# Loading the first tile of a ragged layer norm by a plain GpSimd transfer instead of an indexed gather

## The chip, the cores and the metric

The kernel runs on one core of a Trainium2 chip. Its time is device microseconds (us) of one execution. Before the change, three runs took 264.95, 263.61 and 265.17 us; the median is 264.95 us. The profiled execution is one of them.

The engines are named as in the profile: PE is the matrix engine (TensorE), PEld its weight load, DVE the vector engine, ACT the scalar engine, POOL is GpSimd, SP the sync engine. Sixteen DMA engines move the data between the memory (HBM) and the core's buffers.

## The reference

`x` holds 32 batches of 512 rows of 1,024 float32 values. Of each batch only the first `lengths[b]` rows count (64 to 511, drawn once); they are normalised, scaled by `gamma` and shifted by `beta`, and all other rows of the output are zero.

```python
output = np.zeros_like(x)
for b in range(batch):
    seq_len = lengths[b]
    x_b = x[b, :seq_len].copy()
    mean = np.mean(x_b, axis=-1, keepdims=True)
    var = np.var(x_b, axis=-1, keepdims=True)
    x_norm = (x_b - mean) / np.sqrt(var + eps)
    output[b, :seq_len] = x_norm * gamma + beta
```

## The kernel before

**Units and tiles.** Four consecutive rows of a batch are a unit: 16 KiB, contiguous in memory (`UR = 4`, line 14). A tile is 128 units, one in each partition, 2 MiB. Every batch has at least 64 rows, so the first 16 units of each batch are always valid: these 512 units are the four static tiles (`NST = 4`; tile 0 holds the first 64 rows of batches 0 to 7, `BPT = 8`). The units behind the first 16 of each batch are valid as far as the length says. The kernel counts the valid ones through all batches and packs them densely into dynamic tiles; the units that hold no valid row are packed likewise into zero tiles. The drawn lengths give 1,814 valid dynamic units, so 14 full dynamic tiles and one partial tile with 22 units.

**Loads and stores.** All of them are indirect transfers issued by GpSimd (lines 521, 540 and 547): each of the 128 partitions has the number of its unit in a column of an index tile, and a number out of range is left out. The static tiles take their numbers from `sidx`, which a short chain makes: an iota for the partition number `p_i` and one for the tiles' bases `sb_i` on GpSimd (lines 178 and 179), a shift and a multiply-add on DVE (lines 180 to 184). The dynamic tiles take theirs from `idx_i`, the end of a longer chain on DVE that starts with the lengths (lines 231 to 267). The zero tiles are scattered from one zeroed buffer, `zt`, with numbers from `zidx`. In the partial tile the order of units over the partitions is permuted (lines 202 to 213): the low four bits of a unit's place are bits 2, 3, 4 and 6 of the partition's number.

**The order of work.** The program of each engine is written out by hand: `add` appends an instruction with its semaphore waits, and `raw` appends a marker to GpSimd's list, such as `("load", 0)`. GpSimd's own block (from line 501) walks the list and turns these markers into transfers. It is in order: the two iotas, the loads of tiles 0 and 1, more iotas, the identity's memset, loads 2 to 7, the memset of `zt`. Before load 0 it waits for `sidx` (line 558), before load 4 for `idx_i` and for the number of tiles (lines 559 to 564). After that comes a loop over the tiles: store tile t once it is evacuated, scatter one zero tile at the steps listed in `ZSTEPS`, load tile t + 7 into the buffer that has come free (there are eight buffers, `R = 8`). What zero tiles are left follow at the end.

**The compute** goes by half tiles, two units' rows at a time. DVE takes the statistics from `x` (line 362) and the small reciprocals (lines 352, 353), ACT normalises into a half-precision buffer `h` (line 373), DVE multiplies by gamma (line 346), PE carries `h` over by an identity matrix and adds beta by a rank-one product (lines 398 and 404), ACT evacuates the sum with the row mask into the same `x` buffer (line 382), from which the store goes out.

Of the kernel before, what the change touches and what calls it, by code (L numbers as in the profile page):

```python
# [13 lines left out]
UR = 4  # L14
ST_ROWS = 64
# [6 lines left out]
class Program:  # L22
# [10 lines left out]
    def add(self, eng, fn, deps=(), inc=True):  # L33
        know = self.know[eng]
        waits = {}
        for dep in deps:
            if dep is None:
                continue
            key, val = dep
            if key == eng:  # L40
                waits[key] = max(waits.get(key, 0), val)
                continue
            if know.get(key, 0) >= val:
                continue
            waits[key] = max(waits.get(key, 0), val)
            know[key] = max(know.get(key, 0), val)
            for k2, v2 in self.snap.get(dep, {}).items():
                if k2 != eng:
                    know[k2] = max(know.get(k2, 0), v2)
        own = waits.pop(eng, None)  # L50
        if own is not None and know.get(eng, 0) < own:
            waits[eng] = own
            know[eng] = own
        if inc:
            self.count[eng] += 1
            token = (eng, self.count[eng])
            self.snap[token] = {k: v for k, v in know.items() if k != eng}
        else:
            token = None
        self.ops[eng].append(("op", fn, list(waits.items()), inc))  # L60
        return token
# [8 lines left out]
def kernel(tc, x, lengths, gamma, beta, eps, out):  # L70
# [6 lines left out]
    BPT = B // NST  # L77
# [10 lines left out]
    s_x = [tc.alloc_semaphore(f"s_x{i}") for i in range(R)]  # L88
# [10 lines left out]
    with pool_cm as sb, psum_cm as psb:  # L99
        def st(shape, dt, name):  # L100
            return sb.tile(shape, dt, name=name)

        xt = [st([P, UR * D], FP32, f"x{i}") for i in range(R)]
# [66 lines left out]
        pr = Program(sem)  # L170
        add = pr.add

        def iota(t, pattern, base=0, mult=0):
            return add("POOL", lambda: pool.iota(t, pattern=pattern, base=base, channel_multiplier=mult,
                                                 allow_small_or_imprecise_dtypes=True))


        a_p = iota(p_i[:, :], [[0, 1]], 0, 1)
        a_sb = iota(sb_i[:, :], [[BPT * U, NST]], 0, 1)
        a_p4 = add("DVE", lambda: dve.tensor_scalar(out=p4_i[:, :], in0=p_i[:, :], scalar1=4, scalar2=None,  # L180
                                                    op0=OP.logical_shift_right), [a_p])
        a_sidx = add("DVE", lambda: dve.scalar_tensor_tensor(
            out=sidx[:, :], in0=p4_i[:, 0:1].broadcast_to([P, NST]), scalar=float(U - S0), in1=sb_i[:, :],
            op0=OP.mult, op1=OP.add), [a_p4, a_sb])
        pr.raw("POOL", ("load", 0))
        pr.raw("POOL", ("load", 1))
        a_q = iota(q_f[:, :], [[P, NQ]], 0, 1)
        a_t = iota(t_f[:, :], [[1, NQ]])
# [5 lines left out]
            out=idn_f[:, :], in_=idn_f[:, :], compare_op=OP.not_equal, fill=1.0,  # L194
# [235 lines left out]
        def emit_op(e, name, op):  # L430
            _, fn, waits, inc = op
            for key, val in waits:
                e.wait_ge(handles[key], val)
            ins = fn()
            if inc:
                ins.then_inc(sem[name], 1)
# [8 lines left out]
        def tiles_register(e, r):  # L445

            e.reg_add(r, r, P - 1)
            e.reg_alu(r, r, 7, OP.arith_shift_right)
            e.reg_add(r, r, NST)
# [28 lines left out]
        with tc.tile_critical():  # L478
            with nc.Block() as block:

                @block.vector
                def _(e):
                    run_engine(e, "DVE", block)
# [17 lines left out]
                @block.gpsimd  # L501
                def _(e):
                    base = nc.cur_bb
                    rt = rb = None
                    guard = None

                    def goto(name):
                        nonlocal guard
                        if guard is not None:
                            guard.__exit__(None, None, None)  # L510
                        guard = nc.bb(name, parent=base)
                        guard.__enter__()

                    def wait(dep):
                        e.wait_ge(handles[dep[0]], dep[1])

                    def column(t):
                        return sidx[:, t : t + 1] if t < NST else idx_i[:, t - NST : t - NST + 1]

                    def load(t):  # L520
                        e.indirect_dma_start(
                            out=xt[t % R][:, :], out_offset=None, in_=xu,
                            in_offset=bass.IndirectOffsetOnAxis(ap=column(t), axis=0),
                            bounds_check=B * U - 1, oob_is_err=False).then_inc(s_x[t % R], 16)

                    def guarded_load(t):
                        if t <= NST:
                            load(t)
                            return
                        e.br_lt(rt, t, f"POOL_n{t}", f"POOL_l{t}")  # L530
                        goto(f"POOL_l{t}")
                        if t >= R:
                            wait((f"o{t % R}", 16 * (t // R)))
                        load(t)
                        e.br(f"POOL_n{t}")
                        goto(f"POOL_n{t}")

                    def store(t):
                        wait(tok["evac", 2 * t + 1])
                        e.indirect_dma_start(  # L540
                            out=ou, out_offset=bass.IndirectOffsetOnAxis(ap=column(t), axis=0),
                            in_=xt[t % R][:, :], in_offset=None,
                            bounds_check=B * U - 1, oob_is_err=False).then_inc(s_o[t % R], 16)

                    def zero(j):
                        g = NZ - 1 - j
                        e.indirect_dma_start(  # L547
                            out=ou, out_offset=bass.IndirectOffsetOnAxis(ap=zidx[:, g : g + 1], axis=0),
                            in_=zt[:, :], in_offset=None,
                            bounds_check=B * U - 1, oob_is_err=False).then_inc(s_zero, 16)  # L550

                    for op in pr.ops["POOL"]:
                        if op[0] == "op":
                            emit_op(e, "POOL", op)
                            continue
                        t = op[1][1]
                        if t == 0:
                            wait(a_sidx)
                        if t == NST:
                            wait(d_idx)  # L560
                            rt = units_register(e, "POOL")
                            rb = e.alloc_register("POOL_rb")
                            e.reg_alu(rb, rt, 7, OP.arith_shift_right)
                            tiles_register(e, rt)
                        guarded_load(t)

                    def ready(j):
                        if j == 0:
                            wait(d_zidx)
                            wait(a_zt)  # L570

                    j = 0
                    for t in range(NT):
                        store(t)
                        if t in ZSTEPS and j < NZ:
                            ready(j)
                            e.br_lt(rb, NZ - j, f"POOL_z{t}", f"POOL_y{t}")
                            goto(f"POOL_z{t}")
                            zero(j)
                            e.br(f"POOL_y{t}")  # L580
                            goto(f"POOL_y{t}")
                            j += 1
                        if t >= 1 and t - 1 + R <= NT:
                            guarded_load(t - 1 + R)
                        if t >= NST - 1 and t < NT - 1:
                            e.br_lt(rt, t + 2, f"POOL_e{j}", f"POOL_s{t + 1}")
                            goto(f"POOL_s{t + 1}")
                    e.br(f"POOL_e{j}" if j < NZ else "POOL_exit")
                    for j in range(NZ):
                        goto(f"POOL_e{j}")  # L590
                        ready(j)
                        e.br_lt(rb, NZ - j, f"POOL_t{j}", "POOL_exit")
                        goto(f"POOL_t{j}")
                        zero(j)
                        e.br(f"POOL_e{j + 1}" if j + 1 < NZ else "POOL_exit")
                    goto("POOL_exit")
                    e.drain()
                    e.br(block.end_bb)
                    guard.__exit__(None, None, None)
# [35 lines left out]
```

## Time and profile before

| | |
|---|---|
| median of three runs | 264.95 us |
| profiled execution, in all | 264.95 us |
| span of the profiled execution, first to last instruction | 263.2 us |
| busy: ACT, DVE, PE, POOL | 69%, 67%, 54%, 23% of the span |
| moved by DMA | 105.42 MB in 7,795 packets, 401 GB/s over the span |
| read from and written to HBM | 41.98 MB and 69.21 MB |
| first load, from issue to landing | 8.5 us |
| loads of the second round, from issue to landing | 17.6 to 25.6 us |
| last zero scatter issued | 227.70 us |

The page's second part cuts the span into 40 equal slices, 6.58 us each; a digit is the busy share of that slice in tenths, for the engines and for the mean of the 16 DMA engines. The third part lists the DMA queues with their packets, megabytes and the time that their packets took as a share of 16 engines' span. The timeline lists instructions in order: start, duration, engine, line, operation, output and inputs, and in brackets the idle time of the engine before it and what ended it. A table of stretches gives the busy time of each engine in a part of the span, the granted clock, the share of the DMA engines and GB/s. [...]

### The profile page before, as it was taken

Reading aid. Unit: us, or ns where it says so; the run is one execution under the profiler, and the core shown is the slowest. Engines: PE = TensorE matmul, PEld = TensorE weight load, DVE = VectorE, ACT = ScalarE, POOL = GpSimd, SP = SyncE. Lnnn points to the kernel's source line nnn. Section 1 sums busy time; section 2 is a strip of 40 time slices with the busy share of each in tenths; the row PEclk is TensorE's granted clock in tenths of the full one; section 3 lists DMA queues with packets and bytes.
Section 4 is the critical chain, followed back from the end, with each engine's and each line's share of the span. In section 5 each row is a group of like instructions: output and inputs, shape, how many; then the busy total and the mean of one; then the engine's idle time right before and its main releaser. Section 6 shows DMA issues by size and latency. Waiting matters only on the chain.

```text
span 263.2 us, 1571 instructions
## 1 busy us (share of the span) xinstructions
PE 141.7 (54%) x306; PEld 32.4 (12%) x306; DVE 177.2 (67%) x411; ACT 182.9 (69%) x198; POOL 61.7 (23%) x67
## 2 busy tenths in 40 slices
PE   1006546466687587677767866875876777000000
PEld 0001111111111111111111111111111111000000
DVE  5899796967688778868887886887788688000000
ACT  5144938577989989998998999899899989300000
POOL 5590030315043040302202401240207611200000
DMA  3999999999999999999999999999999999999940
GB/s 111 391 410 406 433 431 431 431 431 433 406 436 408 418 427 421 431 431 428 428 426 426 433 420 423 435 421 428 423 431 428 421 431 416 421 422 426 431 209 10
DMA packets 7795, 105.42 MB, mean 401 GB/s; under 512 B 1356, under 2 KB 1356, under 8 KB 1358
## 3 DMA queue, kind: packets, MB, share of 16 engines
q0 software_dynamic: 7632, 105.22, 95.1%
q8 instruction: 4, 0.07, 0.1%
q14 instruction: 11, 0.09, 0.1%
q10 hardware_dynamic: 148, 0.04, 0.1%
HBM read 41.98 MB, written 69.21 MB: 423 GB/s over the span
## 4 chain that ended last, share of the span: by engine, by line
DVE 35%; PE 27%; ACT 17%; DMA 3%; issue 3%; POOL 0%; ACTq 0%; DVEq 0%; POOLq 0%; SPq 0%
DVE stats_127 L362 17%; PE ps_144 L398 14%; PE ps_144 L404 13%; DMA x_61<-in_x_dram,sidx 3%; DVE h_69 L346 3%; DVE h_71 L346 3%; DVE h_70 L346 3%; ACT x_63 L382 3%; ACT x_62 L382 2%; ACT x_61 L382 2%; ACT x_67 L382 2%; ACT x_68 L382 2%; ACT x_66 L382 2%; ACT x_65 L382 2%; ACT x_64 L382 2%
## 5 line engine op out<-in xcount | busy, mean ns | idle before, releaser
L404 PE MATMUL ps_144<-row_h,ones_h 1*128 1x512 f16 x76 | 35.8, 622 | 0.0
L404 PE MATMUL ps_145<-row_h,ones_h 1*128 1x512 f16 x76 | 35.8, 622 | 0.0
L398 PE MATMUL ps_144<-h_69,idn_h 128*128 128x512 f16 x28 | 13.2, 628 | 26.7 <-DVE h_69 L346 26.7
L398 PE MATMUL ps_144<-h_71,idn_h 128*128 128x512 f16 x24 | 11.3, 627 | 15.5 <-DVE h_71 L346 15.5
L398 PE MATMUL ps_144<-h_70,idn_h 128*128 128x512 f16 x24 | 11.3, 627 | 13.8 <-DVE h_70 L346 13.8
L398 PE MATMUL ps_145<-h_70,idn_h 128*128 128x512 f16 x28 | 13.2, 627 | 6.8 <-DVE h_70 L346 6.8
L346 DVE TENSOR_TENSOR h_69<-h_69,gamma_h 128x2048 f16<-128x2048 f16 x13 | 15.5, 1191 | 1.0 <-ACT x_63 L382 1.0
L547 POOL DMA_INDIRECT out_dram<-zt,zidx x14 | 14.3, 1024 | 5.2 <-issue 3.7
L346 DVE TENSOR_TENSOR h_70<-h_70,gamma_h 128x2048 f16<-128x2048 f16 x13 | 15.4, 1187 | 0.0
L398 PE MATMUL ps_145<-h_71,idn_h 128*128 128x512 f16 x24 | 11.3, 627 | 6.6 <-DVE h_71 L346 6.6
L398 PE MATMUL ps_145<-h_69,idn_h 128*128 128x512 f16 x24 | 11.3, 628 | 6.5 <-DVE h_69 L346 6.5
L346 DVE TENSOR_TENSOR h_71<-h_71,gamma_h 128x2048 f16<-128x2048 f16 x12 | 14.3, 1192 | 0.0
L404 PEld LDWEIGHTS ps_144<-row_h,ones_h 1*128 1x128 f16 x76 | 7.9, 125 | 26.6 <-issue 26.6
L404 PEld LDWEIGHTS ps_145<-row_h,ones_h 1*128 1x128 f16 x76 | 7.9, 125 | 26.6 <-issue 26.6
L352 DVE RECIPROCAL rstd_138<-sq_134 128x2 f32<-128x2 f32 x10 | 1.7, 166 | 13.7 <-ACT sq_134 L389 13.7
L352 DVE RECIPROCAL rstd_136<-sq_132 128x2 f32<-128x2 f32 x10 | 1.7, 166 | 12.9 <-ACT sq_132 L389 12.9
L362 DVE BATCH_NORM_STATS2 stats_126<-x_61 128x6 f32<-128x512 f32 x12 | 7.4, 679 | 0.9 <-DMA x_61<-in_x_dram,sidx 0.9
L398 PEld LDWEIGHTS ps_144<-h_69,idn_h 128*128 128x128 f16 x28 | 3.0, 131 | 36.8 <-DVE h_69 L346 33.0
L362 DVE BATCH_NORM_STATS2 stats_127<-x_63 128x6 f32<-128x512 f32 x12 | 7.4, 680 | 0.0
L362 DVE BATCH_NORM_STATS2 stats_127<-x_62 128x6 f32<-128x512 f32 x12 | 7.4, 679 | 0.0
L362 DVE BATCH_NORM_STATS2 stats_126<-x_64 128x6 f32<-128x512 f32 x12 | 7.4, 679 | 0.0
L362 DVE BATCH_NORM_STATS2 stats_126<-x_62 128x6 f32<-128x512 f32 x12 | 7.4, 678 | 0.0
(181 smaller groups left out, 356.9 us busy)
## 6 DMA issues: line engine op xcount, KB each, us to landing
out_dram<-zt,zidx POOLq DMA_INDIRECT x14, 26.5
len_73<-in_lengths_dram ACTq DMA_DIRECT2D x1, 32.0 KB, 2.9
x_65<-in_x_dram,idx_i POOLq DMA_INDIRECT x2, 22.0
x_66<-in_x_dram,idx_i POOLq DMA_INDIRECT x2, 21.4
x_67<-in_x_dram,idx_i POOLq DMA_INDIRECT x2, 23.9
x_68<-in_x_dram,idx_i POOLq DMA_INDIRECT x2, 25.6
x_61<-in_x_dram,idx_i POOLq DMA_INDIRECT x2, 19.1
x_62<-in_x_dram,idx_i POOLq DMA_INDIRECT x2, 21.0
```

Source lines behind the costliest of these rows:

```text
L346: tok["mul", t] = add("DVE", lambda: dve.tensor_tensor(out=h[:, :, :], in0=h[:, :, :], in1=gamma_h[:, None, :].broadcast_to([P, 2, D]), op ...
L352: a = add("DVE", lambda: dve.reciprocal(out=rstd[r][:, :], in_=sq[r][:, :]), [tok["sqrt", t]])
L362: tk = add("DVE", lambda j=j, c=c: dve.bn_stats(out=s[:, j, c, :], in_=xx[:, j * D + c * CH : j * D + c * CH + CH]), [load_dep(t // 2)])
L382: tok["evac", t] = add("ACT", lambda j=j, row=row: act.activation(out=xx[:, j * D : j * D + D], in_=p_[:, j, :], func=AF.Copy, bias=0.0, s ...
L398: add("PE", lambda j=j, c=c: pe.matmul(p_[:, j, c * CH : c * CH + CH], idn_h[:, :], h[:, j, c * CH : c * CH + CH], start=True, stop=False) ...
L404: tok["pe", t] = add("PE", lambda j=j, c=c: pe.matmul(p_[:, j, c * CH : c * CH + CH], ones_h[:, :], row_h[:, D + c * CH : D + c * CH + CH] ...
L547: e.indirect_dma_start(out=ou, out_offset=bass.IndirectOffsetOnAxis(ap=zidx[:, g : g + 1], axis=0), in_=zt[:, :], in_offset=None, bounds_c ...
```

## The change

The marker `("load", 0)` is moved up between the two iotas, and GpSimd's block issues that load as a plain transfer that takes no indices: the source is the first 64 rows of batches 0 to 7, regrouped into 8 batches of 16 units of 4,096 elements, the destination the whole buffer, 128 partitions. The wait for `sidx` moves from load 0 to load 1. The bytes moved and their places are the same. No other engine's instructions change.

```diff
         a_p = iota(p_i[:, :], [[0, 1]], 0, 1)
+        pr.raw("POOL", ("load", 0))
         a_sb = iota(sb_i[:, :], [[BPT * U, NST]], 0, 1)
         a_p4 = add("DVE", lambda: dve.tensor_scalar(out=p4_i[:, :], in0=p_i[:, :], scalar1=4, scalar2=None,
                                                     op0=OP.logical_shift_right), [a_p])
         a_sidx = add("DVE", lambda: dve.scalar_tensor_tensor(
             out=sidx[:, :], in0=p4_i[:, 0:1].broadcast_to([P, NST]), scalar=float(U - S0), in1=sb_i[:, :],
             op0=OP.mult, op1=OP.add), [a_p4, a_sb])
-        pr.raw("POOL", ("load", 0))
         pr.raw("POOL", ("load", 1))
...
                         t = op[1][1]
                         if t == 0:
+                            e.dma_start(out=xt[0][:, :],
+                                        in_=x[0:BPT, 0:ST_ROWS].rearrange("b (p r) d -> b p (r d)", r=UR)
+                                        ).then_inc(s_x[0], 16)
+                            continue
+                        if t == 1:
                             wait(a_sidx)
                         if t == NST:
                             wait(d_idx)
```

## The prediction

> **What bounds the kernel now.** I read the page from its top. In the second part I look for an engine at 9 in every slice, and in the third at what each queue carries.
>
> ```profile
> DMA  3999999999999999999999999999999999999940
> GB/s 111 391 410 406 433 431 431 431 431 433 406 436 408 418 427 421 431 431 428 428 426 426 433 420 423 435 421 428 423 431 428 421 431 416 421 422 426 431 209 10
> ...
> q0 software_dynamic: 7632, 105.22, 95.1%
> ```
>
> No compute engine does that (ACT, the busiest, is at 69%), but the DMA engines do from the second slice to the 38th, almost all of it in one queue, the one that GpSimd fills. So the time is the start of the transfers, plus the bytes on the engines, plus the end. The price of a tile comes from the last line: 105.22 MB are 6,422 pieces of 16 KiB; 0.951 x 16 x 263.2 us = 4,005 engine-us, hence 0.624 us a piece. A tile of 128 rows is 79.8 engine-us, or 4.99 us when dealt evenly to 16 engines.
>
> The chain that ended last starts with the first tile's load and then walks through DVE, PE and ACT. It must not be taken for the bound: the last store and the last zero scatter are issued at 226.42 and 227.70 us, and the engines still move over 400 GB/s until 251 us. Some 25 us of transfers are waiting in the queue when the compute is done. The start is in the timeline of GpSimd:
>
> ```profile
> 1.06 0.13 POOL L174 IOTA p_i<- 128x1 int32 x1 [0.62 <-SPq L479]
> 1.15 0.12 POOL L174 IOTA sb_i<- 128x4 int32 x1
> 2.62 1.18 POOL L521 DMA_INDIRECT x_61<-in_x_dram,sidx  x1 [1.35 <-DVE one_106 L216]
> 4.11 1.00 POOL L521 DMA_INDIRECT x_62<-in_x_dram,sidx  x1 [0.30 <-issue]
> ```
>
> The first gather is issued at 2.62 us, 0.97 us after its indices are done (DVE writes `sidx` from 1.49 to 1.65). Its issue takes 1.18 us, and it lands 8.5 us after the start of it (sixth part of the page), at 11.13. The end is in stretches of 1 us, where the last two columns are the mean busy share of the 16 engines and GB/s:
>
> ```profile
> 251.00:252.00 1.00, 0.00 (x0) 0.00 (x0) 0.00 (x0) 0.00 (x0) 0.00 (x0) 1.00 0.78 328
> 252.00:253.00 1.00, 0.00 (x0) 0.00 (x0) 0.00 (x0) 0.00 (x0) 0.00 (x0) 1.00 0.61 262
> 253.00:254.00 1.00, 0.00 (x0) 0.00 (x0) 0.00 (x0) 0.00 (x0) 0.00 (x0) 1.00 0.46 197
> 254.00:255.00 1.00, 0.00 (x0) 0.00 (x0) 0.00 (x0) 0.00 (x0) 0.00 (x0) 1.00 0.35 147
> 255.00:256.00 1.00, 0.00 (x0) 0.00 (x0) 0.00 (x0) 0.00 (x0) 0.00 (x0) 1.00 0.08 33
> 256.00:257.00 1.00, 0.00 (x0) 0.00 (x0) 0.00 (x0) 0.00 (x0) 0.00 (x0) 1.00 0.04 16
> ...
> 258.00:259.00 1.00, 0.00 (x0) 0.00 (x0) 0.00 (x0) 0.00 (x0) 0.00 (x0) 1.00 0.04 16
> ```
>
> A share of 0.04 to 0.08 is one engine of sixteen. The engines don't help each other out: from 256 us one of them works alone. The kernel ends with **the most loaded or slowest engine**, not with the mean. The trace's records of the single semaphore increments (each transfer has sixteen) say the same: those of the last scatter arrive from 252.08 to 256.10 us and one, the last, at 259.62; 3.5 us of barrier and exit follow to the span's 263.2.
>
> **The change part by part.** The sum is made against the profiled execution, 263.2 us of span and 264.95 us in all, which is also the median of the runs shown.
>
> (1) *The first load no longer waits for indices.* Both kernels issue it as GpSimd's first transfer; now it follows the `p_i` iota, done at 1.19. How late it starts after that is not shown. The smallest gap ahead of any issue in the timeline is 0.30 us, the gap of the first issue of all is the 0.97 above, part of which may be waiting. So it starts at 1.49 to 2.16 instead of 2.62: 0.46 to 1.13 us gained. I take 0.46, since the row of the first issue is the nearest. The issue of a plain transfer on GpSimd isn't in the trace either: the nearest rows are the gather's 1.18 us and, as ends, 0.23 us (a plain issue on ACT, L490) and 2.00 us (the longest indirect one). I take 1.18, no change; the ends are 0.95 gained and 0.82 lost. Together **-0.46 us**, between -2.08 and +0.36. As the queue is never empty afterwards, the start moves the end by as much.
>
> (2) *`sb_i` is now queued behind the issue on GpSimd*, so it is written near 2.16 + 1.18 = 3.4 us, not 1.15, and `sidx` near 3.7, not 1.49. Behind `sidx` on DVE stand the ten small operations of lines 204 to 216 (1.57 to 2.67 us); they end near 4.8. The lengths' cast follows (3.82 before, 1.0 us later now), and so does the index chain, whose `idx_i` is done at 11.1 in place of 10.09; ACT's first activation waits for one of these constants, `row_h` stands behind it, and `gamma_h` slips with them. Cover: load 1 waits for `sidx` and is issued at 4.0 to 4.6 (4.11 before) while the first tile is still moving; load 4 (11.70 before, it needs `idx_i`) finds loads 1 to 3 queued, 15 us of work; `gamma_h` is first used at 20.70. Cost 0; without the cover of the queue it would be 1.0 us.
>
> (3) *How the tile is dealt to the engines.* The gather takes 128 rows of 16 KiB by index. The plain transfer's source, `x[0:8, 0:64]` regrouped, is a pattern of three dimensions: 8 batches, 16 units in each, 4,096 elements; the batches can't be merged with the units, since 448 rows lie between. No row of before shows a plain transfer of this size. The nearest are ACT's: the lengths' broadcast, 128 rows, goes as 128 packets, while gamma, one row of 4.0 KB, is a single packet on a single engine (the page counts only two packets between 2 and 8 KB: gamma and beta). So a plain transfer is dealt by the shape of its pattern, not by its bytes. Two ends, then: all 128 rows over 16 engines, +0; or the eight outer blocks over eight engines, 16 pieces each. By the second the eight carry 8 pieces more than before, 8 x 0.624 = **+4.99 us**, and the other eight as much less. I take eight, because the outermost dimension is what differs from the gather's pattern, and gamma's row shows that a single outer block isn't split.
>
> [...]
>
> (4) *Whether the last engine is among the eight.* In the code the partial tile's units are permuted (lines 202 to 213), its 22 valid units (the drawn lengths give 1,814, or 14 x 128 + 22) going one to each of sixteen groups of partitions and a second one to the first six. The engine that lands last, at 259.62, took 1.21 us for the store of that tile, two pieces, where ten engines took one; so it is one of the first six, and all partitions of those lie below 64. Eight engines counted from the first would include it. I take that: the whole 4.99 counts.
>
> Load 0 then lands some 5 us later than 2.16 + 8.5, near 15.6, and the compute starts 4.5 us late (first statistics at 11.15 before). That is hidden: the last scatter would be issued at 232 and the queue runs to 264. The queue's smallest stock is ahead of store 1 (47.92), which lands after 13.4 us, 4.99 of them its own: 8.4 us. On the loaded engines stock and issue shift together; the other eight, 5.5 us ahead, may stand for 8.4 - 4.5 - 5.5 = -1.6 us, with 3.9 still in hand. Nothing.
>
> Sum: -0.46 + 0 + 4.99 = **+4.5 us: 269.5 us**, with (1)'s bounds 267.9 to 270.3.
>
> **Rivals.**
> *All sixteen engines carry the tile* (not slower): only (1) and (2) remain, 264.5 us, between 262.9 and 265.3. It decides as soon as the 128 rows, and not the blocks, are dealt out. For it: the destination has 128 rows, as the gather's. Against it: gamma's single packet. The compute wouldn't start earlier even so, since DVE is busy with indices until about 11.2.
> *Eight engines, but not the last one.* It would end 5.5 us early, at 254.2, and the next, 256.10, would end at 256.10 + 4.53 = 260.6, 1.0 us after the old end: 265.9 us.
> *The late indices or the late first tile become the bound.* The last scatter needs about 10 us from issue (8.5 for the first load alone), so it would have to be issued after 250, 22 us later than now. Almost nothing speaks for it. The rest is a plain issue that stalls GpSimd, or some shift in the order of transfers.
>
> **How the numbers follow.** Forecast 0.62, sixteen engines 0.22, eight without the last one 0.12, the rest 0.04. One per cent, 2.65 us, is about what a measurement of this kernel tells from no change. Slower by more: the forecast nearly whole (0.60), 0.01 of the third case, 0.02 of the rest, 0.63. Faster by more: the first rival's far end and the rest's half, 0.05. Within: 0.32. The range goes from 264.2, to take in the third case and half of the second, to 270.5.
>
> **What would show it.** In the GpSimd timeline a plain issue for `x_61` at 1.5 to 2.2 us. In the sixth part its landing: 13 to 14 us after the issue if eight engines carry it, about 8.5 if sixteen do. In the first 10 us a DMA share near 0.5 until load 1's packets come. At the end eight engines, a share near 0.5 or below, for some 8 to 10 us, and no longer a fall over 4 us. I'm wrong if the load lands by 11 us, or if it lands late and the end stays where it was.

## The result and the profile after

| | before | after |
|---|---|---|
| median | 264.64 us | 283.05 us |
| ratio, 95% interval | | 1.0695 (1.0641 to 1.0749) |
| profiled execution, its span | 264.95, 263.2 us | 281.86, 280.1 us |

The change makes the kernel 18.4 us slower: the side that was forecast, at four times the size. First the parts of the page of the changed kernel that were shown of before, and from its sixth part the first load (its size, and us from issue to landing):

```profile
DMA  4999999999999999999999999999999899999960
GB/s 93 154 150 150 365 418 440 421 438 386 400 424 435 395 410 418 442 417 445 419 445 419 433 426 432 426 429 412 405 421 405 363 424 435 421 414 434 421 255 19
...
q0 software_dynamic: 7760, 105.22, 94.7%
...
x_61<-in_x_dram POOLq DMA_DIRECT2D x1, 2048.0 KB, 28.8
```

The bytes are the same. The DMA engines are busy from the start, and yet slices 2 to 4 (7 to 28 us) run at 150 GB/s; before it was 391 to 410. The first load takes 28.8 us in place of 8.5. From slice 6 to the 38th the changed kernel's row runs at 386 to 445 GB/s, much as before, but for a dip at the 32nd (363). The timeline of GpSimd, changed kernel:

```profile
1.06 0.13 POOL L174 IOTA p_i<- 128x1 int32 x1 [0.61 <-SPq L479]
1.63 0.82 POOL L558 DMA_DIRECT2D x_61<-in_x_dram  x1 [0.43 <-issue]
2.46 0.16 POOL L174 IOTA sb_i<- 128x4 int32 x1
3.75 1.08 POOL L521 DMA_INDIRECT x_62<-in_x_dram,sidx  x1 [1.13 <-DVE eps_sb L214]
```

The issue itself does what was hoped for: it starts 0.99 us earlier and takes 0.82 us, not 1.18. The first statistics wait for the load all the same (timeline of DVE, first the kernel before, then the changed kernel; in brackets the idle time before):

```profile
11.15 2.47 DVE L362 BATCH_NORM_STATS2 stats_126<-x_61 128x6 f32<-128x512 f32 x4 [0.93 <-DMA x_61<-in_x_dram,sidx]
30.48 2.47 DVE L362 BATCH_NORM_STATS2 stats_126<-x_61 128x6 f32<-128x512 f32 x4 [19.30 <-DMA x_61<-in_x_dram]
```

What the pieces of 16 KiB cost can be read from a table of stretches: sixteen engines, each with a piece at a time, move share x 16 x 16.384 KB per piece time, so a piece takes share x 262.1 / (GB/s) us. Stretches of the kernel before, last two columns share and GB/s:

```profile
6.00:10.00 4.00, 0.90 (x2) 0.00 (x0) 3.83 (x6) 1.02 (x1) 2.78 (x3) 1.00 0.99 426
```

That is 0.61 us a piece, the commonest duration in that kernel's records too. The changed kernel:

```profile
6.00:10.00 4.00, 1.03 (x2) 0.13 (x2) 3.69 (x9) 1.23 (x2) 2.41 (x3) 1.00 1.12 193
10.00:14.00 4.00, 0.00 (x0) 0.00 (x0) 1.11 (x4) 0.00 (x0) 1.05 (x2) 1.00 0.97 139
14.00:20.00 6.00, 0.00 (x0) 0.00 (x0) 0.00 (x0) 0.00 (x0) 5.39 (x4) 1.00 1.07 164
```

1.5, 1.8 and 1.7 us: while load 0 is under way a piece takes two and a half to three times as long by these shares, on all sixteen engines, load 1's pieces too. The trace's records of single increments show who carries what. (All such times below are on the axis of the timeline.) Of load 0's sixteen, eight arrive at 3.61 to 3.98 us, when nothing has landed, and eight at 29.66 to 30.45: **eight engines carry the tile**. Load 1's arrive at 20.70 to 21.25 on eight engines, which had only its 8 pieces each to do, and at 34.72 to 35.25 on the others. At the end it is still visible (stretches, changed kernel):

```profile
268.00:269.00 1.00, 0.00 (x0) 0.00 (x0) 0.00 (x0) 0.00 (x0) 0.00 (x0) 1.00 0.74 311
270.00:271.00 1.00, 0.00 (x0) 0.00 (x0) 0.00 (x0) 0.00 (x0) 0.00 (x0) 1.00 0.40 164
272.00:273.00 1.00, 0.00 (x0) 0.00 (x0) 0.00 (x0) 0.00 (x0) 0.00 (x0) 1.00 0.31 131
275.00:276.00 1.00, 0.00 (x0) 0.00 (x0) 0.00 (x0) 0.00 (x0) 0.00 (x0) 1.00 0.04 16
```

Of the last scatter's increments eight arrive at 269.06 to 269.23 us, and those of the loaded engines at 271.36 to 276.28. So the question is not whether eight engines carry the tile, but **why a piece costs 1.7 us instead of 0.62**.

### The profile page after: what moved, and what is told of

Same layout as the page of the kernel before. It is cut to its first block, busy times and chain, and to the rows that moved or that the text cites. A ratio compares the mean times of both kernels' runs of the same rounds, so it can differ in the third digit from the quotient of the medians.

```text
span 280.1 us, 1570 instructions
## 1 busy us (share of the span) xinstructions
PE 141.7 (51%) x306; PEld 32.3 (12%) x306; DVE 175.7 (63%) x411; ACT 182.8 (65%) x198; POOL 60.9 (22%) x67
## 4 chain that ended last, share of the span: by engine, by line
DVE 32%; PE 25%; ACT 16%; DMA 10%; issue 3%; POOL 1%; ACTq 0%; DVEq 0%; POOLq 0%; SPq 0%
DVE stats_127 L362 16%; PE ps_144 L398 13%; PE ps_144 L404 12%; DMA x_61<-in_x_dram 10%; DVE h_69 L346 3%; DVE h_71 L346 3%; DVE h_70 L346 3%; ACT x_63 L382 2%; ACT x_61 L382 2%; ACT x_62 L382 2%; ACT x_66 L382 2%; ACT x_65 L382 2%; ACT x_64 L382 2%; ACT x_68 L382 2%; ACT x_67 L382 2%
## 5 line engine op out<-in xcount | busy, mean ns | idle before, releaser
L362 DVE BATCH_NORM_STATS2 stats_126<-x_61 128x6 f32<-128x512 f32 x12 | 7.4, 679 | 19.3 <-DMA x_61<-in_x_dram 19.3
L389 ACT ACTIVATE sq_132<-mv_128,eps_sb 128x2 f32<-128x2 f32 x10 | 2.9, 293 | 24.9 <-DVE mv_128 L367 24.9
L540 POOL DMA_INDIRECT out_dram<-x_61,sidx x1 | 1.0, 1024 | 29.5 <-ACT sq_135 L389 29.5
L362 DVE BATCH_NORM_STATS2 stats_126<-x_62 128x6 f32<-128x512 f32 x12 | 7.4, 678 | 0.0
L362 DVE BATCH_NORM_STATS2 stats_127<-x_62 128x6 f32<-128x512 f32 x12 | 7.4, 679 | 0.0
## 6 DMA issues: line engine op xcount, KB each, us to landing
x_61<-in_x_dram POOLq DMA_DIRECT2D x1, 2048.0 KB, 28.8
```

The lines of the kernel that those rows point to most:

```text
L362: tk = add("DVE", lambda j=j, c=c: dve.bn_stats(out=s[:, j, c, :], in_=xx[:, j * D + c * CH : j * D + c * CH + CH]), [load_dep(t // 2)])
L389: tok["sqrt", t] = add("ACT", lambda: act.activation(out=sq[r][:, :], in_=mv[r][:, :, 1], func=AF.Sqrt, bias=eps_sb[:, 0:1], scale=1.0), [ ...
L540: e.indirect_dma_start(out=ou, out_offset=bass.IndirectOffsetOnAxis(ap=column(t), axis=0), in_=xt[t % R][:, :], in_offset=None, bounds_che ...
```

## The experiments

Three theories at first. A: the eight engines read in step at addresses one batch (2 MiB) apart, and such reads hinder each other. B: it is on the side of the buffers, with the blocks of 16 consecutive partitions that the engines write. C: a plain GpSimd transfer of several blocks is slow in itself. No run so far had shown any of the three.

### Reads one batch apart, by the gather

```diff
...
+        j_f = ((5, OP.logical_shift_left, 7 * U, OP.bitwise_and), (3, OP.logical_shift_right, 12, OP.bitwise_and),
+               (3, OP.bitwise_and, 0, OP.logical_shift_left))
...
+        a_sidx = add("DVE", lambda: dve.tensor_tensor(out=sidx[:, 0:1], in0=j_i[:, 0:1], in1=j_i[:, 2:3],
+                                                      op=OP.bitwise_or), [j_o])
```

> The kernel before, with the indexed gather and all sixteen engines, but the 128 units of tile 0 are dealt to the partitions in another order: each of the sixteen engine groups reads units of one batch, in step, so that pieces read at the same time lie 2 MiB (one batch) apart, as in the changed kernel's plain transfer. Same units, same output. Theory A (reads 2 MiB apart slow each other down): the first load lands 18 to 30 us after its issue in place of 8.5, all engines are late by the same, the total is 10 to 20 us above before. Theory B (the blocks of 16 partitions that eight engines write are what is slow) and theory C (a plain GpSimd transfer of this shape is slow in itself): about 8.5 us to landing, the total +0.5 to +1.5 us, for the five small DVE operations that make the indices.

Measured: ratio 1.0019 (0.9993 to 1.0044). The load runs at full speed (stretches of this kernel):

```profile
6.00:10.00 4.00, 0.62 (x2) 0.00 (x0) 3.83 (x5) 1.02 (x1) 3.09 (x7) 1.00 0.93 389
10.00:14.00 4.00, 0.00 (x0) 0.00 (x0) 2.67 (x8) 0.00 (x0) 1.54 (x3) 1.00 1.03 430
```

0.63 us a piece, at 389 to 430 GB/s: theory A falls. That pieces read at the same time lie a batch apart here is my assumption, from how I took the gather to be dealt (see theory D below); no trace shows it. The next two runs don't need it.

### The same blocks, other distances

```diff
-                                        in_=x[0:BPT, 0:ST_ROWS].rearrange("b (p r) d -> b p (r d)", r=UR)
+                                        in_=xu[0 : BPT * 17, :].rearrange("(b p) f -> b p f", p=17)[:, 0:S0, :]
```

> The changed kernel, with the plain transfer's eight source blocks 17 units (272 KiB) apart instead of one batch (2 MiB); still eight blocks of 16 units to eight engines, still blocks of 16 partitions. Tile 0 then holds other rows, so the output of tile 0 isn't the reference's; the work is the same. Theory A: the first load lands 12 to 14.5 us after its issue (28.8 in the changed kernel) and the total is +3 to +6 us against before, as the prediction had it. Theories B and C: about 28.8 us and +16 to +19 us as in the changed kernel.

> The changed kernel, with the eight source blocks 129 units (2 MiB and 16 KiB) apart: one piece more than a batch. Tile 0 holds other rows, so its output isn't the reference's. Theory A, if what hurts is that the pieces lie a multiple of 2 MiB apart: 12 to 14.5 us to landing, total +3 to +6 us. If what hurts is only that they lie far apart: 28.8 us and +16 to +19. Theories B and C: the same as the latter.

Measured: 1.0687 (1.0663 to 1.0712) at 17 units, 1.0691 (1.0664 to 1.0718) at 129. The page of the run at 17 units, sixth part:

```profile
x<-in_x_dram POOLq DMA_DIRECT2D x1, 2048.0 KB, 29.4
```

The distance in memory makes no difference: 1.0687 and 1.0691 against the changed kernel's 1.0695. The cause lies with the transfer or with what it writes.

### Sixteen blocks

```diff
-                                        in_=x[0:BPT, 0:ST_ROWS].rearrange("b (p r) d -> b p (r d)", r=UR)
+                                        in_=x[0:BPT, 0:ST_ROWS].rearrange("b (p r) d -> p b (r d)", r=UR)
```

and the numbers of tile 0's store set to batch p & 7, unit p >> 3.

> The changed kernel, with the plain transfer's source regrouped to 16 units of 8 batches (units outermost), so the outermost dimension is 16, and the numbers of tile 0's store made to match (three small DVE operations, done long before the store). Same output. Theory A: sixteen engines, each time reading sixteen neighbouring units of one batch; the first load lands 7 to 9 us after its issue, the total is -0.4 to -2 us against before. Theory B: the same or somewhat slower. Theory C: still 20 us or more to landing and +10 us or more.

Measured: 1.012 (1.010 to 1.014), 12.4 us from issue to landing. All sixteen increments arrive together (13.50 to 14.08 us), so all engines carry the tile, evenly; and still:

```profile
6.00:10.00 4.00, 0.78 (x2) 0.00 (x0) 3.69 (x8) 1.02 (x1) 2.37 (x2) 1.00 0.91 197
```

1.21 us, twice the gather's. In the records most pieces of load 0 take 1.13 to 1.28 us, and load 1's, by gather, 0.61. Twice, and in the changed kernel up to three times (the commonest duration there is 1.82 us), looks like streams that share something. This made **theory D**: engines that write to the same group of partitions at the same time share that group's rate. What makes up a group no trace names. I assumed the groups by which the code deals the partial tile (lines 202 to 213), four partitions and the four that lie 32 above, and one engine to each of them in a gather; the counts of the partial tile's pieces fit this (two on six engines, one on ten). If sixteen blocks are dealt in order, engine e has partitions 8e to 8e+7, and in step two engines are always in the same one of these groups.

### One block of 128 rows

```diff
-                                        in_=x[0:BPT, 0:ST_ROWS].rearrange("b (p r) d -> b p (r d)", r=UR)
+                                        in_=xu[0:P, :]
```

> The changed kernel, with the plain transfer reading the 128 consecutive units of batch 0: one outer dimension of 128 rows instead of 8 blocks of 16. Tile 0 holds other rows, so its output isn't the reference's. Theory D (DMA engines that write to the same group of partitions at the same time share that group's rate; the gather's deal gives each engine a group of its own, the deal of a blocked plain transfer doesn't): with 128 rows the deal is the gather's again, pieces take 0.61 us, the load lands 7 to 8.5 us after its issue at 1.6 us, the total is 0 to -2 us against before. Theory C (a plain GpSimd transfer is slow in itself): 11 us or more to landing, +1.5 us or more, as with sixteen blocks.

Measured: 0.9949 (0.9911 to 0.9987), sixth part and stretches of this kernel:

```profile
x<-in_x_dram POOLq DMA_DIRECT2D x1, 2048.0 KB, 8.3
```

```profile
6.00:10.00 4.00, 0.76 (x2) 0.00 (x0) 3.71 (x7) 1.02 (x1) 2.37 (x2) 1.00 0.96 410
```

0.61 us a piece. Theory C is left for sources of several blocks alone: a plain GpSimd transfer is as fast as the gather when its source is a single row of 128 units (8.3 us to landing against 8.5), and it does bring the early start: 1.35 us, by the ratio.

### The eight engines alone

```diff
                         if t == 1:
                             wait(a_sidx)
+                            wait(("x0", 16))
```

> The changed kernel, but GpSimd waits for load 0 to land before it issues load 1, so that the eight engines are alone. Theory D: the eight engines share four groups, two to a group, pieces take 1.22 us, 16 of them 19.6 us: the load lands 20 to 22 us after its issue (28.8 with load 1 beside it). If eight engines on such a transfer are slow for a reason of their own: still 27 to 29 us. The other eight engines do nothing meanwhile; the total isn't what is asked here, about +15 us.

Measured: 284.39 us in one run; load 0's last increment at 23.86 us, 22.2 after the issue at 1.64. Stretches of this kernel:

```profile
10.00:14.00 4.00, 0.00 (x0) 0.00 (x0) 0.00 (x0) 0.00 (x0) 0.00 (x0) 1.00 0.47 106
14.00:20.00 6.00, 0.00 (x0) 0.00 (x0) 0.00 (x0) 0.00 (x0) 0.00 (x0) 1.00 0.52 117
```

Half of the engines are busy (share 0.47 to 0.52), and a piece takes 1.16 to 1.17 us, where theory D, with two streams to a group, expected 1.22. The landing is 0.2 us later than expected; the first piece of each engine takes 1.5 to 2.2 us. What a piece takes beyond this in the changed kernel, up to 1.5 to 1.8 us, comes with load 1 beside it.

### Neighbours in groups of their own

```diff
...
-                            e.dma_start(out=xt[0][:, :],
-                                        in_=x[0:BPT, 0:ST_ROWS].rearrange("b (p r) d -> b p (r d)", r=UR)
+                            e.dma_start(out=xt[0][0:64, :],
+                                        in_=x[0:BPT, 0 : ST_ROWS // 2].rearrange("b (p r) d -> b p (r d)", r=UR)
...
+                        if t == 1:
+                            e.dma_start(out=xt[0][64:P, :], in_=xu[0:64, :]).then_inc(s_h, 16)
```

> The changed kernel, with the plain transfer cut to the lower 64 partitions (8 blocks of 8 units, still eight engines) and a second plain transfer of 64 consecutive units for the upper 64 partitions behind load 1. Tile 0 holds other rows, so its output isn't the reference's. Engines that aren't loaded by the first transfer write load 1's rows to the upper 64 partitions, groups that the first transfer doesn't touch. Theory D, with the rate shared in a group and nowhere else: the other eight engines do their pieces of load 1 at 0.61 us and are done with them by 12 us, and the eight pieces of load 0 take 1.22 us each, landing 10 to 12 us after issue. Theory E (one crowded group holds up the other transfers too, beyond its own partitions): the other eight engines take 1.2 us or more a piece and are done after 15 us.

Measured: 277.77 us in one run. The other eight engines start load 1 at 6.1 to 6.7 us, and their increments come at 15.58 to 15.79, 1.2 us for each of eight pieces; in the records the eighth piece alone is at 0.61, when load 0 has landed (13.53 to 14.65). Stretches of this kernel:

```profile
6.00:10.00 4.00, 0.87 (x2) 0.00 (x0) 3.72 (x7) 1.02 (x1) 3.08 (x5) 1.00 1.05 233
10.00:14.00 4.00, 0.00 (x0) 0.00 (x0) 0.92 (x4) 0.00 (x0) 1.59 (x3) 1.00 0.97 217
```

So it is theory E: the crowd doesn't stay among those who share a group. By the assumed deal the other engines' rows go to partitions 64 to 127, which load 0 doesn't touch here, and their pieces take twice as long too, 1.2 us against 0.61. (That the loaded engines are the first eight is seen in the changed kernel: all six that take two pieces of the partial tile are among those that run late.) By what path they are held up no run shows. It would also give the changed kernel's price, as an estimate that no run separates: there, by the assumed groups, two of the four that load 0's engines write at a time lie in partitions 64 to 127, where the other eight write load 1. So three streams meet in these, and 3 x 0.61 = 1.83 is close to the commonest duration, 1.82 us, that engines of both halves show.

### Four transfers, two orders

```diff
...
-                            e.dma_start(out=xt[0][:, :],
-                                        in_=x[0:BPT, 0:ST_ROWS].rearrange("b (p r) d -> b p (r d)", r=UR)
-                                        ).then_inc(s_x[0], 16)
+                            for i, c in enumerate((0, 2, 1, 3)):
+                                e.dma_start(out=xt[0][32 * c : 32 * c + 32, :],
+                                            in_=x[0:BPT, 16 * c : 16 * c + 16].rearrange("b (p r) d -> b p (r d)", r=UR)
+                                            ).then_inc(s_x[0] if i == 3 else s_h, 16)
```

The other order is `(0, 1, 2, 3)`; tile 0's store numbers are batch (p >> 2) & 7, unit 4 (p >> 5) + (p & 3).

> The changed kernel, with load 0 in four plain transfers of 32 partitions, each of 8 blocks of 4 units (8 batches, one block each, so eight engines to a transfer and one block of four partitions to an engine), in the order partitions 0-31, 64-95, 32-63, 96-127; the numbers of tile 0's store are made to match. Same output. Theory D: if consecutive transfers of eight blocks go to the two halves of the engines in turn, every engine has a group of partitions of its own, as with the gather: pieces take 0.61 us, all four have landed by 10 to 11 us, the total is 0 to -2 us against before. If all four go to the same eight engines: 16 pieces of 0.61 each on those, landed by 13 to 15 us, total +3 to +5 us. Theory C (blocked plain transfers are slow whatever the partitions): over +10 us.

> The same as the run before, in the order of the partitions: 0-31, 32-63, 64-95, 96-127. Same work, same number of transfers, same output; but now the first two transfers, on the two halves of the engines, write the same eight groups, then the last two. Theory D: two engines to a group, pieces take 1.22 us in place of 0.61; all landed by 13 to 15 us, the total is +1 to +4 us against before, as with sixteen blocks. If the order didn't matter: as the run before.

Measured: **0.9955 (0.9928 to 0.9982)** for the first order, 1.005 (1.0019 to 1.008) for the second. Only the order of two transfers differs. The stretches, first of the order 0, 2, 1, 3:

```profile
6.00:10.00 4.00, 1.03 (x2) 0.13 (x2) 3.65 (x11) 2.49 (x2) 3.04 (x10) 1.00 1.02 385
```

then of 0, 1, 2, 3:

```profile
6.00:10.00 4.00, 1.03 (x2) 0.13 (x2) 3.65 (x11) 2.50 (x2) 3.05 (x10) 1.00 1.04 291
```

0.69 against 0.94 us a piece; the last increments of the quarters come at 11.49 and 13.44 us. So partitions 0 to 31 written beside 32 to 63 hinder each other, and beside 64 to 95 hardly: this much of the assumed groups is shown. In the second order the pieces go back and forth between 0.61 and 1.2 us: the two halves of the engines started 1.5 us apart, so by theory D they meet in a group only part of the time, and the total came out just at the low end of what was expected. That consecutive transfers of eight blocks take the two halves of the engines in turn is seen in the first order: had the same eight carried everything, it would have landed at 13 to 15 us, as the expectation has it, and not at 11.49. The first order is faster than both kernels: by about 1.2 us than before, by about 20 us than the changed one. With it theory C falls for sources of several blocks too.

### Four engines to a group

```diff
...
-                            e.dma_start(out=xt[0][:, :],
-                                        in_=x[0:BPT, 0:ST_ROWS].rearrange("b (p r) d -> b p (r d)", r=UR)
-                                        ).then_inc(s_x[0], 16)
+                            for i in range(BPT):
+                                e.dma_start(out=xt[0][i * S0 : (i + 1) * S0, :], in_=xu[i * U : i * U + S0, :]
+                                            ).then_inc(s_x[0] if i == BPT - 1 else s_h, 16)
```

> The changed kernel, with load 0 in eight plain transfers, one a batch: 16 units to 16 consecutive partitions, 16 engines with one piece each. Same output. The 16 engines write four groups at a time, four engines to a group. Theory D with the engines in step: pieces take 2.4 us, eight of them 19.5 us, and load 0 has landed by 22 to 25 us, total +9 to +14 us against before, spread evenly over the engines. If the engines drift apart and spread over the groups, less: down to 14 us and +3. If sharing a group cost nothing: landed by 10 to 11 us, total within 2 us.

Measured: 1.040 (1.0348 to 1.0452); load 0's last increment at 21.85 us. Stretches of this kernel:

```profile
6.00:10.00 4.00, 0.90 (x2) 0.12 (x2) 3.51 (x23) 2.09 (x2) 2.38 (x9) 1.00 1.12 131
10.00:14.00 4.00, 0.12 (x1) 0.00 (x0) 3.86 (x6) 1.02 (x1) 1.75 (x2) 1.00 1.12 131
```

2.24 us by the shares; in the records seven pieces of each engine take 2.19 to 2.21 us, as even as that. The engines keep step, each of the assumed groups has four streams, and a piece takes 3.6 times 0.61. Evenly spread over the engines, it still costs 10 us. The reads can't be the cause of this: here, as with the sixteen blocks, the sixteen engines read the first sixteen units of one batch at a time, and only the partitions that they write differ, for 2.2 us a piece against 1.21.

| streams in a group at a time, by the assumed groups | kernel | a piece |
|---|---|---|
| 1 | before, one block of 128 rows | 0.61 us |
| 2 | sixteen blocks; eight engines alone | 1.21; 1.16 to 1.17 |
| 4 | batch by batch | 2.2 |
| 2, by the deal 3 in some groups, with eight other engines at work | after | 1.5 to 1.8 |

### The early start without a plain transfer

```diff
+        for i in range(4):
+            a_sidx = iota(sidx[32 * i : 32 * i + 32, :], [[4, NST]], i, U)
+        pr.raw("POOL", ("load", 0))
         a_p = iota(p_i[:, :], [[0, 1]], 0, 1)
-        a_sb = iota(sb_i[:, :], [[BPT * U, NST]], 0, 1)
...
```

> The kernel before with gathers only, but the static tiles are made up differently (tile t holds units 4t to 4t+3 of all 32 batches, one unit number to each 32 partitions), so that GpSimd itself writes all indices by four iotas and load 0 doesn't wait for DVE. Same output. All theories: the deal to the engines is the gather's, pieces take 0.61 us; the load is issued at 1.9 to 2.3 us instead of 2.62 and lands 8 to 9 us later; the total is 0 to -1 us against before, by the engines' reads being one batch apart no slower (the first run with reads one batch apart was not).

Measured: 1.0028 (0.9993 to 1.0062), no gain. Timeline of GpSimd of this kernel:

```profile
1.06 0.70 POOL L174 IOTA sidx<- 32x4 int32 x4 [0.62 <-SPq L477]
2.73 1.17 POOL L519 DMA_INDIRECT x<-in_x_dram,sidx  x1 [0.96 <-POOL sidx L174]
```

The indices are ready at 1.76 us, written by GpSimd itself, and the gather starts 0.97 us later, as it did before behind DVE. The gap goes with the indexed transfer, not with the other engine; ahead of the plain one it is 0.43. In all these runs this transfer is both the first indexed one and the first to use new indices; which of the two makes the gap no run separates.

## Why the prediction was right or wrong

**The bound** was read rightly: the queue. The last scatter is issued 16.9 us later than before (first line before, second after), and its last increment follows 31.7 us after that in both kernels:

```profile
227.70 0.98 POOL L547 DMA_INDIRECT out_dram<-zt,zidx  x1 [0.30 <-issue]
244.61 0.97 POOL L547 DMA_INDIRECT out_dram<-zt,zidx  x1 [0.30 <-issue]
```

The last to end is one of the loaded engines. (The prediction's times of single increments at the end, 252.08 to 259.62 us, are 0.24 us late against the axis of its other lines: the last one is at 259.38, and 3.8 us follow it. Its sum doesn't use the difference.)

**Step (1)** had the right sign, and taking the near row made it too small: the start moved by 0.99 us, where 0.46 was taken and 1.13 was the bound, and the issue by 0.36 us, where nothing was taken. Together -1.35 us, within -2.08 to +0.36. The 0.97 us gap is no price of a first issue of any kind, as I took it for: it stood ahead of the first indexed transfer, and the plain one's was 0.43.

**Step (2)** held. `sidx` was done at 2.83 us, before the 3.7 given, load 1 was issued at 3.75, `idx_i` was done at 11.05 (11.1 given) and load 4 issued at 12.64. Load 1 did wait for `sidx`, and was still issued 0.36 us earlier than before.

**Step (3)**, in its first half, was right: eight engines, sixteen pieces each. **Its price was the error.** "8 x 0.624" takes the piece time of the gather into a transfer that is dealt otherwise. The 0.624 us was no property of an engine; by theory D it was that of a deal in which no two engines write to the same group, and under the other deals a piece took 1.16 to 2.2 us. By the records a piece of load 0 took 1.6 us on average on the loaded engines, and from the first piece at 3.15 to the last increment at 30.45 it took 27.3 us. Before, load 0's pieces began at 4.51 and its last increment came at 11.13: 6.6 us. So the transfer grew by 20.7 us, where the step had 4.99; less the 1.36 by which it began earlier, the load landed 19.3 us later. Of this 16.9 are left at the end. The missing 2.4 are about what the last engine's lag behind the next one shrank by, from 3.5 to 1.3 us; why it shrank no run shows.

**Step (4)** was right: the engines that take two pieces of the partial tile are all among the loaded eight.

**What was said to hide** was hidden on the loaded engines, though the compute began 19.3 us late and not 4.5. The other eight engines did run dry, at another place than the one that was worked out: at 214 to 220 us, with a share of 0.80, when GpSimd's issues waited for a store to land. It cost nothing at the end, as they were ahead.

**The rivals.** "All sixteen engines" was worked out at 264.5 us with the gather's price again; sixteen blocks on sixteen engines came out at +1.2%, because the price had doubled, and the 128 rows and the first order of the four transfers gave what that rival promised. So none of the three answers on the engines' number was enough: each asked how many engines, none where they write. That the deal could change the price of every piece, load 1's included, was in neither forecast nor range.

## What to carry to other kernels

The time of a piece in the profile belongs to the deal that it was measured under. Before pricing a transfer of another shape, ask which engines carry it and which partitions each of them writes at the same time: here a plain transfer whose source had 8 outer blocks was carried by eight engines, at 1.16 to 1.17 us a piece alone and 1.5 to 1.8 with a second load beside it, whose pieces were as slow; with 16 blocks a piece took 1.21 us on sixteen engines. By theory D, engines in step meet in the same groups of partitions. A single outer dimension of 128 rows ran at 0.61 us a piece, and transfers of 32 partitions in eight blocks of four rows, alternating between the lower and the upper 64, at 0.69; the latter gains 0.45% on the kernel before.

## What the runs showed of the hardware that I had not expected

- A piece of 16 KiB took 0.61 us in the gather and in the block of 128 rows, 1.16 to 1.21 where the assumed groups have two streams each, 2.2 where they have four.
- Eight engines that write blocks of the lower 64 partitions hold up eight others that, by the assumed deal, write elsewhere: 1.2 us a piece instead of 0.61. The path is open.
- A gather whose reads in step, by the assumed deal, lie one batch (2 MiB) apart ran at 389 to 430 GB/s in the first load, where the kernel before had 426 (6 to 10 us).
- The first indexed GpSimd transfer started 0.92 to 0.97 us after its indices were written, whether DVE wrote them or GpSimd itself; a plain one started 0.43 us after the iota ahead of it.
- Of the changed kernel's first load, which eight engines carry, eight increments arrive at 3.61 to 3.98 us, 26 us ahead of the other eight (29.66 to 30.45): only the full sixteen say that it has landed.
